# Two-layer hybrid decoder on one core: the SSM preparation's product on four column strips, and its kept matrices turned by DVE squares and DMAs instead of PE

## The chip, the cores and the metric

One core of a Trainium2 chip runs the whole kernel in one launch. The metric is the device time of that launch in microseconds, the median of three runs before. TensorE (PE) does the matmuls and has its own queue of weight loads (PEld); VectorE (DVE), ScalarE (ACT) and GpSimd (POOL) do the rest; SyncE (SP) issues nearly all DMAs. Each engine takes its instructions in the order in which they were emitted.

## What is computed

Two layers on x of 256 positions by 2048 columns. Each layer: RMSNorm, one input projection (2048 to 2816), three token mixers side by side, an output projection, a residual, RMSNorm, a SwiGLU feed-forward network of width 5632, a residual. The mixer that matters here is the SSM:

```
# per group g (32 groups of 16 channels, 64 complex states each)
s_t = Abar s_{t-1} + Bbar u_t          # Abar, Bbar from lam, dt, b only: no x in them
y_t = Re(C s_t) + D u_t
y   = gelu(y);  y = y * sigmoid(y @ w_glu)
```

## The kernel before

**Matmuls.** All large products are float32 split into two float32r parts. Weights stream from DRAM in 684 halves of 128x1024 (512 KB each) through five buffers ("raw"). ACT rounds a half to "whi" (L193), DVE makes the rest "wlo" (L203), and `unit` (L285 to L287) issues for each block of 128 input columns and each of two position blocks three matmuls of 512 columns: whi by xh, wlo by xh, whi by xl. A half is used up in two units.

**The order of the work.** One program order is written out in Python. `dense` emits one unit and then calls `tick` once. A tick gives each of the small tasks (generators) at most one step, six tasks per tick at most, the oldest first; `yield 0` means "go on at the next tick", `yield n` means n ticks later than that. Where a dense product needs something that a task has not emitted yet, `need` calls `tick` again and again with no dense unit between: below these are called empty ticks. The order in each engine's queue follows from this, and waits between engines are semaphores that the framework puts in.

**The SSM preparation, `ssm_prep(l, ct)`.** For each layer and each of four quarters ct of the groups it makes a "stash" of 3584 columns: wr and wi (each 512: block matrices turned by PE), m (512: the product of spread B and C powers, Toeplitz in blocks of four positions), gr, gn, cos, sin, d0. The turns are four PE transposes each (`turn`, L588), copied out by ACT at L622 and L637. The product is eight matmuls (L643) with 32 output rows each, `ps[0:32]`, at four column offsets, in two ticks of four; ACT then makes m with four copies (L651), shifted by 32 columns for each block of 32 rows. Only one preparation runs at a time (`prep_busy`).

Layer 0 prepares quarter 3 first and keeps it in DRAM (`saved`, L655), then quarters 0, 1 and 2, which stay in SBUF, all while the input projection runs. The four of layer 1 are prepared in the feed-forward network of layer 0, spaced by yields of 12 ticks (`slow`), and all kept in DRAM. `ssm_load` (L543) brings a kept stash back with one DMA of 1792 KB. So five of eight preparations are kept, and three are not.

**What uses the stash, `ssm_main(l, ct)`.** Eight matmuls with wr and wi (L683), DVE products and scans (L691 to L709), 12 matmuls with m, gr, gn (L716, L719, L721; float32, so each is two records in the trace), DVE (L728), gelu on ACT (L733), DVE squares (L736). Its yields add up to 19 ticks. `ssm_one` starts it when its preparation is done; quarter 3 is loaded when quarter 0's main is through.

**What waits for that.** The stash of quarter 1 lies in the buffer "ya" and that of quarter 2 in "yb". The attention task allocates "ya" for the output projection's input only when `main_done[1]` holds, so the first tile of the output projection follows the main of quarter 1 by four ticks. After four such tiles (16 units), `need(tssm)` at L1140 waits for all four mains and `glu_T`. The six input products before take 16 + 8 + 4 x 16 = 88 units.

Of the kernel before, what the change touches and what calls it, by code (L numbers as in the profile page):

```python
# [10 lines left out]
F32 = mybir.dt.float32  # L11
F32R = mybir.dt.float32r
AF = mybir.ActivationFunctionType
ALU = mybir.AluOpType

L = 2
# [142 lines left out]
class Builder:  # L159
# [380 lines left out]

    def ssm_load(self, l, ct):
        st = self.stash[(l, ct)] = self.ssm_store(ct)
        self.nc.sync.dma_start(out=st["all"], in_=self.saved[l][ct])  # L543
        yield 2

    def load_bc(self):
# [5 lines left out]
    def ssm_prep(self, l, ct, save=None):  # L552
        nc = self.nc
        v, pool = nc.vector, nc.gpsimd
        s0 = 16 * l + 4 * ct
        while self.prep_busy or not self.small_done:
            yield 0
        self.prep_busy = True
        st = self.stash[(l, ct)] = self.ssm_store(ct if save is None else 0 if l else 2)
        bc = self.bc  # L560
        slow = 12 if l else 0
        geng = pool if l else v
        c3 = lambda t, n: t[:, s0:s0 + 4].unsqueeze(2).to_broadcast([128, 4, n])
        v3 = lambda t: t.rearrange("p (a b) -> p a b", b=64)
        it = self.iota.unsqueeze(1).to_broadcast([128, 4, 64])
        cs = st["cs"]

        def cmul(eng, out, t, ar, pr, ai, pi, op, nq):

            sh = [128, 4, nq, 16]  # L570
            t, o = [z[:, 0:64 * nq].rearrange("p (a q b) -> p a q b", q=nq, b=16) for z in (t, out)]
            e = lambda a: a.unsqueeze(2).to_broadcast(sh)
            f = lambda p: p[:, s0:s0 + 4].unsqueeze(3).to_broadcast(sh)
            eng.tensor_tensor(out=t, in0=e(ai), in1=f(pi), op=ALU.mult)
            eng.tensor_tensor(out=o, in0=e(ar), in1=f(pr), op=ALU.mult)
            eng.tensor_tensor(out=o, in0=o, in1=t, op=op)

        def spread(out, src, n):

            o = out.rearrange("p (a b) -> p a b", b=32)  # L580
            i = src[:, 0:16 * n].rearrange("p (a b) -> p a b", b=16)
            for h in range(2):
                nc.scalar.activation(out=o[:, :, 16 * h:16 * h + 16], in_=i, func=AF.Copy, scale=self.half[:, h:h + 1])

        def turn(et):
            ps = yield from self.grab("side")
            for g in range(4):
                nc.tensor.transpose(ps[:, 128 * g:128 * g + 128], et[:, 128 * g:128 * g + 128], self.ident)  # L588
            return ps


        bb = self.work.tile([128, 2, 4, 16], F32, tag="bb", name="bb", bufs=1)
        t4 = st["gn"][:, 320:384].rearrange("p (a b) -> p a b", b=16)
        for o, p, q, op in ((0, 0, 1, ALU.subtract), (1, 1, 0, ALU.add)):
            pool.tensor_tensor(out=bb[:, o], in0=bc[:, p], in1=c3(self.cre, 16), op=ALU.mult)
            pool.tensor_tensor(out=t4, in0=bc[:, q], in1=c3(self.cim, 16), op=ALU.mult)
            pool.tensor_tensor(out=bb[:, o], in0=bb[:, o], in1=t4, op=op)
        cmul(pool, st["d0"], st["wi"][:, 256:512], bb[:, 0], self.per, bb[:, 1], self.pei, ALU.subtract, 4)
        yield 0
        cmul(geng, st["m"], cs, bc[:, 2], self.pfr, bc[:, 3], self.pfi, ALU.subtract, 5)  # L600
        cmul(pool, st["wr"], st["gn"], bc[:, 2], self.pfn, bc[:, 3], self.pfr, ALU.subtract, 5)
        cmul(pool, st["wi"][:, 0:256], st["wi"][:, 256:512], bb[:, 1], self.per, bb[:, 0], self.pei, ALU.add, 4)
        yield 1 + slow
        spread(st["gr"], st["m"], 20)
        yield 0
        et = self.work.tile([128, 512], F32, tag="et", name="et", bufs=1)
        spread(et, st["d0"], 16)
        f, g, h = cs[:, 256:512], cs[:, 0:256], st["m"][:, 0:256]
        v.tensor_tensor(out=v3(f), in0=c3(self.phh, 64), in1=it, op=ALU.mult)
        v.tensor_tensor(out=v3(g), in0=c3(self.phl, 64), in1=it, op=ALU.mult)  # L610
        yield 0
        ps = yield from turn(et)
        v.tensor_tensor(out=h, in0=f, in1=g, op=ALU.add)
        v.tensor_scalar(out=h, in0=h, scalar1=MAGIC, scalar2=MAGIC, op0=ALU.add, op1=ALU.subtract)
        yield slow
        spread(st["gn"], st["wr"], 20)
        self.load_bc()
        v.tensor_tensor(out=f, in0=f, in1=h, op=ALU.subtract)
        v.tensor_tensor(out=f, in0=f, in1=g, op=ALU.add)
        v.scalar_tensor_tensor(out=g, in0=f, scalar=-1.0, in1=f, op0=ALU.mult, op1=ALU.max)  # L620
        yield 0
        nc.scalar.activation(out=st["wr"], in_=ps, func=AF.Copy)  # L622
        self.drop("side")
        et = self.work.tile([128, 512], F32, tag="pt", name="et", bufs=1)
        spread(et, st["wi"], 16)
        yield 0
        nc.scalar.activation(out=st["sin"], in_=f, func=AF.Sin, scale=SIN_SCALE)
        nc.scalar.activation(out=st["cos"], in_=g, func=AF.Sin, scale=-SIN_SCALE, bias=self.hpi)
        yield slow
        ps = yield from turn(et)  # L630
        brep = self.work.tile([128, 2, 4, 32], F32, tag="et", name="brep", bufs=1)
        spread(brep.rearrange("p o a b -> p (o a b)"), bb.rearrange("p o a b -> p (o a b)"), 8)
        pool.memset(st["m"], 0.0)
        pool.tensor_copy(out=v3(st["d0"]), in_=c3(self.rho4, 64))
        pool.memset(v3(st["d0"])[:, :, 0:1], 0.0)
        yield 0
        nc.scalar.activation(out=st["wi"], in_=ps, func=AF.Copy)  # L637
        self.drop("side")
        yield slow
        ps = yield from self.grab("side")  # L640
        for g in range(4):
            for o, nm in ((0, "gr"), (1, "gn")):
                nc.tensor.matmul(out=ps[0:32, 128 * g:128 * g + 128], lhsT=brep[:, o, g],  # L643
                                 rhs=st[nm][:, 160 * g:160 * g + 128], start=(o == 0), stop=(o == 1))
            if g % 2:
                yield 0
        mv = st["m"].rearrange("p (g c) -> p g c", g=4)
        pv = ps.rearrange("p (g c) -> p g c", g=4)
        for q in range(4):
            p0 = 32 * q  # L650
            nc.scalar.activation(out=mv[p0:p0 + 32, :, p0:128], in_=pv[0:32, :, 0:128 - p0], func=AF.Copy)  # L651
        self.drop("side")
        if save is not None:
            yield 0
            nc.sync.dma_start(out=save, in_=st["all"])  # L655
        self.prep_busy = False
        yield 1

# [361 lines left out]
    def build(self):  # L1020
        nc = self.nc
# [50 lines left out]
        def prep0():  # L1072
            yield 15
            nc.vector.tensor_scalar(out=self.nsinks, in0=self.sinks, scalar1=-1.0, scalar2=None, op0=ALU.mult)
            nc.vector.tensor_scalar(out=self.sinks8, in0=self.sinks, scalar1=8.0, scalar2=None, op0=ALU.mult)
            yield from self.ssm_small()
            self.small_done = True
            yield from self.ssm_prep(0, 3, save=self.saved[0][3])

        self.saved = [[self.dram.tile([128, 3584], F32, name=f"saved{l}{ct}", tag=f"saved{l}{ct}") for ct in range(4)]  # L1080
                      for l in range(L)]
        self.spawn(prep0())

        for l in range(L):
# [30 lines left out]
            a = self.acc()  # L1115
            self.dense(a, self.X, D16, ready=ready)
            self.spawn(self.attn(l, 0, a, rs))
            a = self.acc()
            self.dense(a, self.X, D16, n=256)
            self.spawn(self.kv(a, rs))  # L1120
            a = self.acc()
            self.dense(a, self.X, D16)
            self.spawn(self.attn(l, 1, a, rs))
            a = self.acc()
# [3 lines left out]
            a = self.acc()  # L1128
            self.dense(a, self.X, D16)
            self.spawn(self.gmlp_v(l, a, rs))  # L1130
            a = self.acc()
# [6 lines left out]
            for t in out_tiles():  # L1138
                if t is None:
                    self.need(tssm)  # L1140
                    a = []
# [9 lines left out]
                f = n not in accs  # L1151
# [14 lines left out]
            for si, s in enumerate(FF_SETS):  # L1166
                self.hev = self.events()
                for i, c in enumerate(s):
                    a = self.acc()
                    self.dense(a, self.X, D16, ready=ready)  # L1170
                    tgte = self.spawn(self.ffn_h(c, i, a, None, rs))
                    a = self.acc()
# [10 lines left out]
                for n, part in down_parts(s):  # L1183
                    a = accs[n] if n in accs else self.acc()
# [57 lines left out]
        for m in range(2):  # L1242
            r = nrm["rs"][:, m:m + 1]
            t = self.work.tile([128, 2], F32, tag="ms", name="ms", bufs=4)
# [42 lines left out]
```

## Time and profile before

| | |
|---|---|
| median of 3 runs | 2032.88 us (2028.57, 2032.88, 2033.66) |
| the profiled execution | 2028.85 us, span 2027.1 us |
| PE busy, weight loads busy | 2003.0 us, 1668.5 us |
| DVE, ACT, POOL busy | 1201.4, 995.6, 155.9 us |

Busy time of PE contains the overlap of pipelined matmuls, so a matmul that lasts 0.39 us in the trace starts 0.23 us after the one ahead of it. Stages of the profiled execution: mixers of layer 0 up to about 230 us, feed-forward network up to about 1033 us, mixers of layer 1 up to about 1240 us, then the output projection and the second network.

### The profile page before, as it was taken

To read this page: it belongs to the slowest core of one execution; us is meant where nothing else is said; L and a number is where in the kernel's file an instruction comes from. 1 tells how busy PE (TensorE), PEld (TensorE's weight loads), DVE (VectorE), ACT (ScalarE), POOL (GpSimd) and SP (SyncE) were. 2 spreads that over 40 slices of the span, in tenths; PEclk is the share of its full clock that TensorE was granted. 3 is DMA by queue.
4 is the path that set the end of the run, shared out by engine and by line. 5 is a ranking of instruction groups with operands and counts; after the bars stand their busy time and mean duration, and the time that the engine had idled before them with its cause. 6 is when DMAs were issued, how large, how long until landed. Compare 5 with 4: busy or idle time off the path is not lost.

```text
span 2027.1 us, 25451 instructions
## 1 busy us (share of the span) xinstructions
PE 2003.0 (99%) x9456; PEld 1668.5 (82%) x9456; DVE 1201.4 (59%) x1673; ACT 995.6 (49%) x1367; POOL 155.9 (8%) x204
## 2 busy tenths in 40 slices
PE   8999999999999999999999999999999999999998
PEld 7888888888888888888888888888888888888886
DVE  6868775555546555455675796655555555555555
ACT  6776554545445444444455445544443444434443
POOL 0342003020303000000000010000000000000000
PEclk9999999999999999999999999999999999999999
DMA  7533477666656666566776356766665666666664
GB/s 251 174 131 138 154 256 232 222 229 224 223 202 232 235 226 204 193 218 211 252 254 231 108 197 207 240 221 215 216 211 196 208 219 217 213 192 201 225 218 146
DMA packets 127773, 422.63 MB, mean 208 GB/s; under 512 B 15008, under 2 KB 31008, under 8 KB 126368
## 3 DMA queue, kind: packets, MB, share of 16 engines
q1 hardware_dynamic: 125632, 416.69, 61.2%
q0 software_dynamic: 1152, 3.15, 0.6%
q8 instruction: 74, 1.21, 0.2%
q10 hardware_dynamic: 864, 1.16, 0.2%
q14 instruction: 51, 0.42, 0.1%
HBM read 391.84 MB, written 29.10 MB: 208 GB/s over the span
## 4 chain that ended last, share of the span: by engine, by line
PE 94%; DVE 3%; ACT 1%; issue 1%; DMA 1%; SPq 0%; POOLq 0%; POOL 0%; DVEq 0%; ACTq 0%
PE acc L285 29%; PE acc L287 29%; PE acc L286 29%; PE side L909 1%; DVE wlo L203 1%; PE side L643 1%; PE side L683 1%; PE side L875 1%; PE side L899 0%; PE side L349 0%; PE side L721 0%; PE side L719 0%; DVE st L691 0%; PE side L716 0%; PE side L588 0%
## 5 line engine op out<-in xcount | busy, mean ns | idle before, releaser
L203 DVE TENSOR_TENSOR wlo<-raw,whi 128x1024 fp32r<-128x1024 f32 (+1 forms) x687 | 846.1, 1240 | 629.3 <-ACT whi L193 625.4
L193 ACT ACTIVATE whi<-raw 128x1024 fp32r<-128x1024 f32 (+1 forms) x687 | 724.8, 1056 | 957.3 <-PE acc L287 901.7
L285 PE MATMUL acc<-whi,xh 128*128 128x512 f32 (+1 forms) x1792 | 699.9, 391 | 2.9 <-ACT whi L193 1.8
L287 PE MATMUL acc<-whi,xl 128*128 128x512 f32 (+1 forms) x1792 | 692.1, 386 | 0.0
L286 PE MATMUL acc<-wlo,xh 128*128 128x512 f32 (+1 forms) x1792 | 691.8, 386 | 0.1
L285 PEld LDWEIGHTS acc<-whi,xh 128*128 128x128 f32 x1792 | 337.1, 188 | 69.5 <-ACT whi L193 2.2
L287 PEld LDWEIGHTS acc<-whi,xl 128*128 128x128 f32 x1792 | 337.0, 188 | 68.5
L286 PEld LDWEIGHTS acc<-wlo,xh 128*128 128x128 f32 x1792 | 337.3, 188 | 65.2 <-DVE wlo L203 0.8
L285 PE MATMUL acc<-whi,ya 128*128 128x512 f32 x512 | 200.5, 392 | 0.0
L286 PE MATMUL acc<-wlo,ya 128*128 128x512 f32 x512 | 199.3, 389 | 0.3 <-DVE wlo L203 0.3
L287 PE MATMUL acc<-whi,ya 128*128 128x512 f32 x512 | 199.3, 389 | 0.0
L285 PE MATMUL acc<-whi,yb 128*128 128x512 f32 x448 | 175.0, 391 | 0.0
L287 PE MATMUL acc<-whi,yb 128*128 128x512 f32 x448 | 174.4, 389 | 0.0
L286 PE MATMUL acc<-wlo,yb 128*128 128x512 f32 x448 | 174.3, 389 | 0.0
L286 PEld LDWEIGHTS acc<-wlo,ya 128*128 128x128 f32 x512 | 96.2, 188 | 20.2 <-DVE wlo L203 0.7
L287 PEld LDWEIGHTS acc<-whi,ya 128*128 128x128 f32 x512 | 96.1, 188 | 20.1
L285 PEld LDWEIGHTS acc<-whi,ya 128*128 128x128 f32 x512 | 96.2, 188 | 19.7 <-issue 0.2
L287 PEld LDWEIGHTS acc<-whi,yb 128*128 128x128 f32 x448 | 84.1, 188 | 17.6
L285 PEld LDWEIGHTS acc<-whi,yb 128*128 128x128 f32 x448 | 84.1, 188 | 17.4 <-issue 0.2
L286 PEld LDWEIGHTS acc<-wlo,yb 128*128 128x128 f32 x448 | 84.1, 188 | 17.3
L1248 POOL TENSOR_TENSOR rs<-ms,nh 128x1 f32<-128x1 f32 x2 | 1.8, 924 | 699.9 <-DVE ms L1246 699.9
L371 POOL DMA_DIRECT2D turned<-turn x24 | 13.5, 564 | 511.5 <-DVE turn L366 511.4
(251 smaller groups left out, 1196.5 us busy)
## 6 DMA issues: line engine op xcount, KB each, us to landing
raw<-wts SPq DMA_DIRECT2D x684, 512.0 KB, 4.2
quad<-turned SPq DMA_DIRECT2D x34, 512.0 KB, 5.0
turned<-turn SPq DMA_DIRECT2D x112, 128.0 KB, 3.9
saved<-stash SPq DMA_DIRECT2D x4, 1792.0 KB, 6.7
stash<-saved SPq DMA_DIRECT2D x3, 1792.0 KB, 7.6
stashb<-saved SPq DMA_DIRECT2D x2, 1792.0 KB, 9.3
turned<-turn POOLq DMA_DIRECT2D x24, 128.0 KB, 3.9
saved<-stashb SPq DMA_DIRECT2D x1, 1792.0 KB, 6.6
```

The costliest lines, as they stand in the source:

```text
L193: self.nc.scalar.activation(out=h[:, o:o + w], in_=self.raw[j][:, o:o + w], func=AF.Copy)
L203: self.nc.vector.tensor_tensor(out=o[:, i:i + w], in0=r[:, i:i + w], in1=self.hi[j][:, i:i + w], op=ALU.subtract)
L285: nc.tensor.matmul(out=o, lhsT=a, rhs=wh, start=first, stop=False)
L286: nc.tensor.matmul(out=o, lhsT=a, rhs=wl, start=False, stop=False)
L287: nc.tensor.matmul(out=o, lhsT=b, rhs=wh, start=False, stop=last)
L371: queue.dma_start(out=d[:, :, a].rearrange("b j f -> j b f"), in_=t[32 * a:32 * a + 32].rearrange("p (b f) -> p b f", b=4))
L643: nc.tensor.matmul(out=ps[0:32, 128 * g:128 * g + 128], lhsT=brep[:, o, g], rhs=st[nm][:, 160 * g:160 * g + 128], start=(o == 0), stop=(o ...
L683: nc.tensor.matmul(out=ps[:, 256 * o + 64 * g:256 * o + 64 * g + 64], lhsT=st[nm][:, 128 * g:128 * g + 128], rhs=U4[:, 4 * ct + g, :])
L875: nc.tensor.matmul(out=ps[:, nk * i:nk * i + nk], lhsT=qT[:, h0 + i], rhs=self.kT[:, j, cq, 0:nk], start=(j == 0), stop=(j == 1))
L909: nc.tensor.matmul(out=ps[:, 64 * i:64 * i + 64], lhsT=pT[:, 128 * (nb * i + b):128 * (nb * i + b) + 128], rhs=self.v[:, b, 64 * cq:64 * c ...
L1248: nc.gpsimd.tensor_tensor(out=r, in0=t[:, 0:1], in1=self.nh[:, 0:1], op=ALU.pow)
```

## The change

The product's four blocks of rows go to PSUM partitions 0, 32, 64 and 96 (`ps[32g:32g+32, 0:128]`), first all four with gr, then all four with gn, in one tick. One ACT copy of 128x128 moves the result into columns 96 to 223 of m, whose first 96 columns are zero. Four DMAs write it to DRAM, each read from a place shifted by 32 columns, so that the shift of m arises there; for an unkept quarter one more DMA brings m back into SBUF, and the preparation waits four ticks longer for that. For a kept quarter PE does not turn wr and wi: DVE turns 32x32 squares (one instruction of 128x512 each), and eight DMAs, two ticks apart, put blocks of squares in their places in DRAM; gr to d0 go with one DMA as before. `ssm_load` takes three DMAs: two for wr and wi out of the turned blocks, one for the rest.

```diff
 def ssm_load(self, l, ct):
     st = self.stash[(l, ct)] = self.ssm_store(ct)
-    self.nc.sync.dma_start(out=st["all"], in_=self.saved[l][ct])
+    save, turns = self.saved[l][ct]
+    for o in range(2):
+        self.nc.sync.dma_start(out=st["all"][:, 512 * o:512 * o + 512],
+                               in_=turns[o].rearrange("c (q g) s -> q c (g s)", q=4))
+    self.nc.sync.dma_start(out=st["all"][:, 1024:3584], in_=save)
     yield 2
 ...
     def turn(et):
+        if save is not None:
+            return None
 ...
+    def turned(nm, ps, et):
+        if save is None:
+            nc.scalar.activation(out=st[nm], in_=ps, func=AF.Copy)
+            self.drop("side")
+            return
+        v.transpose(out=st[nm].rearrange("p (q g j) -> p g q j", q=4, g=4),
+                    in_=et.rearrange("p (g q j) -> p g q j", g=4, q=4))
 ...
-        nc.scalar.activation(out=st["wr"], in_=ps, func=AF.Copy)
-        self.drop("side")
+        turned("wr", ps, et)
 ...
-        pool.memset(st["m"], 0.0)
+        pool.memset(st["m"][:, 0:96], 0.0)
 ...
-        nc.scalar.activation(out=st["wi"], in_=ps, func=AF.Copy)
+        turned("wi", ps, et)
+        yield slow
+        ps = yield from self.grab("side")
+        for o, nm in ((0, "gr"), (1, "gn")):
+            for g in range(4):
+                nc.tensor.matmul(out=ps[32 * g:32 * g + 32, 0:128], lhsT=brep[:, o, g],
+                                 rhs=st[nm][:, 160 * g:160 * g + 128], start=(o == 0), stop=(o == 1))
+        yield 0
+        nc.scalar.activation(out=st["m"][:, 96:224], in_=ps[:, 0:128], func=AF.Copy)
         self.drop("side")
-        yield slow
-        ps = yield from self.grab("side")
-        for g in range(4):
-            for o, nm in ((0, "gr"), (1, "gn")):
-                nc.tensor.matmul(out=ps[0:32, 128 * g:128 * g + 128], lhsT=brep[:, o, g],
-                                 rhs=st[nm][:, 160 * g:160 * g + 128], start=(o == 0), stop=(o == 1))
-            if g % 2:
-                yield 0
-        mv = st["m"].rearrange("p (g c) -> p g c", g=4)
-        pv = ps.rearrange("p (g c) -> p g c", g=4)
+        yield 1
+        if save is None:
+            rows = self.dram.tile([128, 512], F32, tag="rows", name="rows", bufs=2)
+        else:
+            save, turns = save
+            rows = save[:, 0:512]
         for q in range(4):
-            p0 = 32 * q
-            nc.scalar.activation(out=mv[p0:p0 + 32, :, p0:128], in_=pv[0:32, :, 0:128 - p0], func=AF.Copy)
-        self.drop("side")
-        if save is not None:
-            yield 0
-            nc.sync.dma_start(out=save, in_=st["all"])
+            nc.sync.dma_start(out=rows[32 * q:32 * q + 32].rearrange("c (g t) -> g c t", g=4),
+                              in_=st["m"][:, 96 - 32 * q:224 - 32 * q])
+        if save is None:
+            yield 2
+            nc.sync.dma_start(out=st["m"], in_=rows)
+        else:
+            for o in (0, 512):
+                for a in range(4):
+                    nc.sync.dma_start(out=turns[o // 512][:, :, 32 * a:32 * a + 32],
+                                      in_=st["all"][32 * a:32 * a + 32, o:o + 512].rearrange("c (r j) -> c r j", j=32))
+                    yield 1
+            nc.sync.dma_start(out=save[:, 512:2560], in_=st["all"][:, 1536:3584])
         self.prep_busy = False
         yield 1
```

## Rows read from the trace of the kernel before

**Rows 1.** The page: busy time by engine, granted clock, chain that ended last.

```profile
PE 2003.0 (99%) x9456; PEld 1668.5 (82%) x9456; DVE 1201.4 (59%) x1673; ACT 995.6 (49%) x1367; POOL 155.9 (8%) x204
...
PEclk9999999999999999999999999999999999999999
...
PE 94%; DVE 3%; ACT 1%; issue 1%; DMA 1%; SPq 0%; POOLq 0%; POOL 0%; DVEq 0%; ACTq 0%
```

**Rows 2.** Windows by stage: length, busy time by engine, clock, DMA share, GB/s.

```profile
60.00:205.00 145.00, 138.39 (x837) 117.51 (x836) 111.84 (x269) 104.44 (x217) 45.72 (x65) 1.00 0.43 146
...
355.00:700.00 345.00, 345.00 (x1559) 283.19 (x1559) 190.03 (x190) 171.75 (x218) 50.45 (x66) 1.00 0.66 224
```

**Rows 3.** Timeline of PE around one turn: start, length, engine, line, operation.

```profile
402.68 0.39 PE L287 MATMUL acc<-whi,xl 128*128 128x512 f32 x1
402.91 0.60 PE L588 MATMUL side<-ident,et 128*128 128x128 f32 x4
403.27 0.48 PE L285 MATMUL acc<-whi,xh 128*128 128x512 f32 x1
403.58 0.40 PE L286 MATMUL acc<-wlo,xh 128*128 128x512 f32 x1
```

**Rows 4.** Timeline of PE around one half of the product.

```profile
422.21 0.39 PE L287 MATMUL acc<-whi,xl 128*128 128x512 f32 x1
...
422.53 1.06 PE L643 MATMUL side<-stash,brep 128*32 128x128 f32 x8
...
423.52 0.50 PE L285 MATMUL acc<-whi,xh 128*128 128x512 f32 x1
...
423.86 0.40 PE L286 MATMUL acc<-wlo,xh 128*128 128x512 f32 x1
```

**Rows 5.** Lines L588 and L643: count, shortest, median and longest, first and last.

```profile
L588 PE MATMUL side<-ident,et x64: 270/272/328, 71.7 to 666.4; 128*128 128x128 f32 x64
...
L643 PE MATMUL side<-stash,brep x80: 272/273/297, 116.2 to 689.1; 128*32 128x128 f32 x80
```

**Rows 6.** Timeline of PE where the output projection of layer 0 begins.

```profile
190.00 1.89 PE L683 MATMUL side<-U,stashb 128*128 128x64 f32 x16
...
193.02 0.55 PE L349 MATMUL side<-ident,yattn 128*128 128x128 f32 x3 [0.71 <-ACT yattn L779]
193.40 1.06 PE L958 MATMUL side<-t,wst 128*128 128x128 f32 x8
194.29 1.04 PE L349 MATMUL side<-ident,yattn 128*128 128x128 f32 x8
196.06 1.97 PE L683 MATMUL side<-U,stash 128*128 128x64 f32 x16 [0.73 <-DVE ya L431]
197.84 0.48 PE L285 MATMUL acc<-whi,ya 128*128 128x512 f32 x1
```

**Rows 7.** Groups by line: DVE's squares, count, busy us, mean ns, idle before.

```profile
L366 DVE STREAM_TRANSPOSE turn<-t 128x512 f32<-128x512 f32 x44 | 28.5, 684 | 0.0
```

**Rows 8.** Timeline of PE: half of a main's second product.

```profile
181.92 0.39 PE L716 MATMUL side<-U,stashb 128*128 128x64 f32 x2
...
183.24 0.48 PE L285 MATMUL acc<-whi,xh 128*128 128x512 f32 x1
```

**Rows 9.** DMA issues: count, KB each, median us from issue to landing.

```profile
raw<-wts SPq DMA_DIRECT2D x684, 512.0 KB, 4.2
...
turned<-turn SPq DMA_DIRECT2D x112, 128.0 KB, 3.9
saved<-stash SPq DMA_DIRECT2D x4, 1792.0 KB, 6.7
stash<-saved SPq DMA_DIRECT2D x3, 1792.0 KB, 7.6
```

**Rows 10.** Timeline of SP: layer 1's load of quarter 3 is issued.

```profile
1180.93 0.42 SPq L543 DMA_DIRECT2D stash<-saved  x1
```

**Rows 11.** Timeline of PE: layer 1's main of quarter 3 begins.

```profile
1189.65 1.89 PE L683 MATMUL side<-U,stash 128*128 128x64 f32 x16
```

More of the change, by code (lines that the diff above doesn't have):

```diff
@@ L636, in ssm_prep @@
         yield 0
-        nc.scalar.activation(out=st["wi"], in_=ps, func=AF.Copy)
-        self.drop("side")
+        turned("wi", ps, et)
         yield slow
         ps = yield from self.grab("side")
-        for g in range(4):
-            for o, nm in ((0, "gr"), (1, "gn")):
-                nc.tensor.matmul(out=ps[0:32, 128 * g:128 * g + 128], lhsT=brep[:, o, g],
+        for o, nm in ((0, "gr"), (1, "gn")):
+            for g in range(4):
+                nc.tensor.matmul(out=ps[32 * g:32 * g + 32, 0:128], lhsT=brep[:, o, g],
                                  rhs=st[nm][:, 160 * g:160 * g + 128], start=(o == 0), stop=(o == 1))
-            if g % 2:
-                yield 0
-        mv = st["m"].rearrange("p (g c) -> p g c", g=4)
-        pv = ps.rearrange("p (g c) -> p g c", g=4)
-        for q in range(4):
-            p0 = 32 * q
-            nc.scalar.activation(out=mv[p0:p0 + 32, :, p0:128], in_=pv[0:32, :, 0:128 - p0], func=AF.Copy)
-        self.drop("side")
-        if save is not None:
-            yield 0
-            nc.sync.dma_start(out=save, in_=st["all"])
+        yield 0
+        nc.scalar.activation(out=st["m"][:, 96:224], in_=ps[:, 0:128], func=AF.Copy)
+        self.drop("side")
+        yield 1
[4 more added lines that the diff above has]
+            rows = save[:, 0:512]
+        for q in range(4):
+            nc.sync.dma_start(out=rows[32 * q:32 * q + 32].rearrange("c (g t) -> g c t", g=4),
[10 more added lines that the diff above has]
+            nc.sync.dma_start(out=save[:, 512:2560], in_=st["all"][:, 1536:3584])
         self.prep_busy = False
@@ L1078, in prep0, with kept @@
             yield from self.ssm_prep(0, 3, save=self.saved[0][3])
-        self.saved = [[self.dram.tile([128, 3584], F32, name=f"saved{l}{ct}", tag=f"saved{l}{ct}") for ct in range(4)]
-                      for l in range(L)]
+        def kept(l, ct):
+            a = self.dram.tile([128, 2560], F32, name=f"saved{l}{ct}", tag=f"saved{l}{ct}")
+            b = self.dram.tile([2, 32, 16, 128], F32, name=f"turns{l}{ct}", tag=f"turns{l}{ct}")
+            return a, b
+        self.saved = [[kept(l, ct) for ct in range(4)] for l in range(L)]
         self.spawn(prep0())
```

## The prediction, made before the change was run

> **What bounds the kernel now.** I read the page first: PE is busy for 99% of the span at the full granted clock, and 94% of the chain that ended last is PE, while DVE is busy for 59% and ACT for 49% [rows 1]. The windows by stage come next, and there the reader is to see two different stages. In the feed-forward network of layer 0 (355 to 700 us, where the four preparations of layer 1 run) PE is never idle, so each microsecond of its work that goes is a microsecond of the span. In the mixers of layer 0 (60 to 205 us, where the four preparations of layer 0 run) PE is idle for 145.0 - 138.4 = 6.6 us, and DVE and ACT are busy for more than 70% [rows 2]; there work is bound by chains as well. The third view is the timeline of PE around the edited operations, and the fourth that of the place where the output projection begins.
>
> **Turns that go (five preparations, two each).** Matmuls of 512 columns start 0.23 us apart. The turn lets the next one start at 403.27, where 402.91 would have been its time, so 0.36 us; the one behind it then starts 0.31 instead of 0.23 us later, since its weights were not loaded ahead: 0.08 more [rows 3]. A turn costs 0.44 us of PE. Eight of the ten lie in the network: 8 x 0.44 = 3.5 us. The two of layer 0 give 0.9 us.
>
> **The product (eight preparations).** Half of it is eight records between 422.21 and 423.52, 1.31 us where 0.23 is usual, and the next start is again 0.34 instead of 0.23 us later: 1.08 + 0.11 = 1.19 us per half, 2.38 us per preparation [rows 4]. The eight records span 1.06 us, of which the last takes 0.27 by itself [rows 5], so they start (1.06 - 0.27)/7 = 0.11 us apart and fill 0.88 us; 0.31 us of a half is entering and leaving that form of tile. The new product has 16 records in one group, so 0.31 is paid once. No row shows matmuls on two strips side by side, because all records of before write the same 32 rows. The bounds: nothing overlaps, 0.31 + 16 x 0.11 = 2.07 us, a gain of 0.31; or four strips at once, 0.31 + 4 x 0.11 = 0.75 us, a gain of 1.63. I take a value between: a float32 matmul is two records on the same strip, the second has to follow the first, and starts are in order, so if strips do run beside each other only the second record of one pair and the first of the next can share the time. That is nine steps, 0.31 + 9 x 0.11 = 1.30 us, a gain of 1.08 us per preparation. Four in the network: 4.3 us (1.2 to 6.5). Four in layer 0: the same.
> The Trainium skill, page "TensorE: Matmul & The Clock Gate", section "Part 3: Packing small matmuls", gives 2.38 times for three strips with 512 columns; by that, as an estimate, the 16 records would fill 0.74 us and the gain would be 1.33 us. No row here shows it.
>
> **The network as a whole.** PE gains 3.5 + 4.3 = 7.8 us there (4.7 to 10.0). What hides the new work: two DVE squares of 0.68 us per preparation [rows 7] against two ACT copies that go, on a DVE that is busy 190 of 345 us [rows 2]; a remainder that comes 1 us late still has the two halves of weights (2 x 2.72 us) that DVE works ahead. The DMAs on SP: four of 64 KB for m and eight of 64 KB in pieces of 128 bytes, two ticks (2.72 us) apart. A DMA of 128 KB in pieces of 1 KB lands in 3.9 us [rows 9]; the new ones have half the bytes and four times the pieces, so between 3.9 us and, by pieces alone, 15.6 us. I take the low end, nearest in bytes. A weight half behind one on SP lands in 4.2 us, while five buffers give 5 x 2.72 = 13.6 us; that is the cover, and without it each late half would cost what exceeds 9.4 us. The preparations end 4 x 16 ticks later (87 us), long before layer 1 loads them. So nothing is added here.
>
> **Layer 0, where the change also makes a chain longer.** Counting yields: quarter 3 frees the next preparation 3 ticks after its product before, and 19 after the change (ACT, two ticks, eight DMAs two ticks apart): +16. Quarters 0 and 1 each finish 4 ticks later (the store of m, three ticks, the load). The main of quarter 1 starts when its preparation is done, so it and `main_done[1]` come 16 + 4 + 4 = 24 ticks later. The first tile of the output projection waits for that already: before, nine empty ticks lie between the last unit on X and the first on ya, and they take 197.84 - 190.00 = 7.84 us, 0.87 us each. They hold 52 records (two first products of mains, 12 turns, of which the rows show eleven, and eight of L958) x 0.11 = 5.7 us of PE work, so PE loses only 2.1 us [rows 6]. After the change there are 33 empty ticks. At 0.87 us they last 28.7 us; I take 30, since the chain in them now holds a DRAM round trip (its price is with the rivals). But the work in them is work taken out of the units before: 48 records of L683, 72 of the second products (12 in 183.24 - 181.92 = 1.32 us, 0.11 each [rows 8]), 8 of turns, 28 as before, 156 x 0.11 = 17.2 us, and two products of 1.30: 19.8 us. PE loses 30 - 19.8 = 10.2 us, 8.1 more than before. The units ahead become lighter, and I give back half of the 6.6 us of idle PE [rows 2]: 3.3. Net +4.8 us. The gains of layer 0 are 0.9 + 4.3 = 5.2 us. Layer 0 thus comes out at -0.4 us. The second wait, at `need(tssm)`, moves along: its last main is then 28 ticks later, four more than the first tile, against six empty ticks now, in which other work has gone; I cost it at nothing. The round trip of m (3.9 us to land and, as an estimate, as much to come back) lies within the ticks that I counted; for quarter 2 five units cover it.
>
> **The sum.** -7.8 - 0.4 = -8.2 us. Against the profiled execution's own 2028.85 us that is 2020.7; that execution is one of the fast ones and lies 4.0 us below the median of three, whose runs differ by 5.1 us. Against the median: 2024.7 us.
>
> **The rivals.**
> *Strips run one after another.* The product gains 0.31 eight times, 2.5 instead of 8.6 us: -2.1 us, 2030.8 us, no measurable change. For it: records of one strip do follow at 0.11 us. Against it: those had no choice.
> *The empty ticks fill up.* If the 30 us shrink to the 20 us of work in them, PE loses nothing there: -8.2 - 10.2 = -18 us, about 2014 us. For it: before, 5.7 of 7.84 us were work. Against: the chain alternates DVE, PE and ACT with one quarter left in flight.
> *The load on few rings.* The load of wr and wi now reads DRAM in an outer dimension of four. If transfers are dealt out by it, each of four rings carries 128 KB for wr and wi where the whole old load put 112 KB on each of 16, and 208 KB with the rest: 7.6 us x 208/112 = 14.1 us [rows 9]. In layer 1 quarter 3's main starts 8.7 us after its load was issued [rows 10, 11], so PE waits 0 to 5.4 us: up to 2030.1 us, no measurable change. The Trainium skill, page "DMA: Bandwidth & Descriptors", section "Why a DMA increments its semaphore by 16 and not by 1", has this rule: the number of engines is the largest that divides the slowest dimension of both sides. No row here shows it.
> *Slower: the longer chain in layer 0.* Place: the empty ticks before the first output tile. If one costs 1.36 us, as much as a unit, instead of 0.87, the wait is 45 us, PE loses 15 us more than I take, and the sum is +6.8 us: 2039.7 us. It becomes slower than before once an empty tick exceeds (30 + 8.2)/33 = 1.16 us. For it: the chain now holds a DRAM round trip, which empty ticks of before do not, and SP waits for its landing. Against it: before's ticks held two mains as well.
>
> **How the numbers follow.** About 0.3% (6.1 us) is what a measurement can tell from no change. The forecast with its neighbours 0.48, strips one after another 0.15, the ticks filled 0.10, the few rings 0.10, slower 0.12, and 0.05 for a loss below 6.1 us by the same chain. Faster by over 0.3%: most of the forecast's own cases and the filled ticks, 0.55. Within 0.3%: the serial strips, the few rings, the small loss and what of the forecast falls short of 6.1 us, 0.33. Slower: 0.12. The range takes in the filled ticks, the strips in a row and the small loss, over runs that differ by 5 us: 2013 to 2037.
>
> **What would show it.** L588 falls from 64 to 24 records; L643 stays at 128, in groups of 16 that take about 1.3 us of PE from the last dense matmul to the next, not 2.07 or 0.75. The 355 to 1033 us stage becomes 7.8 us shorter. At the first output tile PE's timeline shows some 30 us without a dense matmul, two thirds of it busy. The prediction is wrong if that gap passes 38 us, if weight halves land late in the network, or if PE waits there for DVE.

## The result: slower by 0.9%, and the profile after

The changed kernel takes 2051.36 us (median of 6 runs, 2048.67 to 2055.16) against 2033.21 us of the kernel before on the same chip (6 runs): a ratio of 1.0093 [1.0082, 1.0104], 18 us more, where 8 us less was forecast. The profiled execution took 2048.67 us, with a span of 2046.7 us.

Of the page of the changed kernel, the rows that answer to [rows 1]:

```profile
PE 2004.7 (98%) x9416; PEld 1671.1 (82%) x9416; DVE 1209.9 (59%) x1683; ACT 984.7 (48%) x1336; POOL 151.6 (7%) x204
...
PEclk9997799999999999999999999999999999999999
...
PE 92%; DVE 3%; ACT 2%; DMA 1%; issue 1%; SPq 1%; POOL 0%; POOLq 0%; DVEq 0%; ACTq 0%
```

PE has 40 records fewer and is busy 1.7 us longer; the reason stands in the row of the clock: in the fourth and fifth slice the granted clock, which was full everywhere before, is at 0.7. To see where the time lies, the start of the k-th dense unit after is set against that of the k-th before. A dense unit is counted here as the three matmuls of one position block (half of what `unit` emits), from 0:

| dense unit | stage | after minus before, us |
|---|---|---|
| 176 | input projection of layer 0, its last tenth | -19.4 |
| 192 | first unit of the output projection | +31.9 |
| 400 | feed-forward network begins | +25.9 |
| 900 | in the network | +15.0 |
| 1000 | end of the network | +17.2 |
| 1570 | layer 1, after quarter 3's main | +19.5 |
| 2767 | end | +20.4 |

So there are four places: layer 0 loses 25.9 us, the network gains 10.8 up to unit 900 and gives back 2.2 behind it, layer 1 loses 1.9 at quarter 3. The rest (1.3 us) is less than runs of one kernel differ by.

**Layer 0.** Busy time from 60 us to unit 400, a windows row of before and then the same of after (columns as in [rows 2]):

```profile
60.00:349.40 289.40, 282.69 (x1502) 237.64 (x1501) 209.22 (x418) 181.30 (x328) 70.50 (x94) 1.00 0.54 179
```

```profile
60.00:375.20 315.20, 293.46 (x1496) 248.31 (x1495) 212.85 (x420) 179.66 (x317) 67.49 (x94) 0.92 0.53 169
```

PE idles 315.20 - 293.46 = 21.7 us where it idled 6.7: 15.0 of the 25.8 us. The other 10.8 are busy time: six records fewer, and yet 10.8 us more. A windows table of the stretch between the last unit on X and the first on ya shows why:

```profile
160.00:170.00 10.00, 9.19 (x80) 8.24 (x79) 6.99 (x17) 6.51 (x12) 5.55 (x12) 1.00 0.25 80
170.00:180.00 10.00, 2.25 (x11) 1.64 (x9) 7.92 (x27) 7.67 (x19) 3.68 (x7) 0.57 0.12 39
180.00:190.00 10.00, 9.36 (x74) 8.68 (x75) 6.61 (x20) 6.60 (x16) 0.00 (x0) 0.75 0.16 36
190.00:200.00 10.00, 6.67 (x33) 6.04 (x31) 4.96 (x20) 7.31 (x12) 1.27 (x1) 0.59 0.83 247
200.00:210.00 10.00, 5.80 (x26) 5.61 (x26) 8.26 (x16) 1.15 (x2) 5.47 (x3) 0.50 0.09 34
210.00:220.00 10.00, 8.69 (x40) 8.51 (x40) 8.78 (x27) 1.45 (x3) 0.00 (x0) 0.50 0.01 2
220.00:230.00 10.00, 8.81 (x41) 8.19 (x41) 5.53 (x17) 4.73 (x10) 0.70 (x1) 0.53 0.00 0
```

From 170 us, where PE was busy for 2.25 us of ten, the granted clock is between 0.75 and 0.50; 0.50 is the lower level, 1.2 GHz. From 210 to 230 us PE is busy for 87% with some 40 records in 10 us, where [rows 6] has 52 in 7.84. The timeline of PE in the same gap of after, with the idle time before an instruction and its releaser in brackets:

```profile
194.24 3.62 PE L708 MATMUL side<-U,stashb 128*128 128x64 f32 x16
...
205.16 0.63 PE L741 MATMUL side<-U,stashb 128*128 128x64 f32 x2
210.74 0.69 PE L744 MATMUL side<-stashb 128*128 128x63 f32 x2 [4.95 <-DVE stashb L716]
...
223.14 2.02 PE L983 MATMUL side<-t,wst 128*128 128x128 f32 x8
...
229.69 0.47 PE L285 MATMUL acc<-whi,ya 128*128 128x512 f32 x1
```

L708 is the old L683 and L983 the old L958: sixteen records take 3.62 us where [rows 6] has 1.89, eight take 2.02 where it has 1.06. The gap lasts from 162.6 to 229.69 us, 67.1 us with 284 records; before it was 7.84 us with 52. What PE waited for in it (total, times, longest):

```profile
PE side L934 <- DVE pT L929: 6.2, 3, 2.9
PE side L594 <- ACT et L587: 5.5, 1, 5.5
PE side L744 <- DVE stashb L716: 4.9, 1, 4.9
PE side L349 <- ACT yattn L804: 1.2, 2, 0.6
```

These are a preparation (L594), a main (L744) and the attention (L934): parts of three chains, each handing over between PE, ACT and DVE. None of them waits for a DMA.

**The network.** A product there, timeline of PE, to be set beside [rows 4]:

```profile
768.15 0.39 PE L287 MATMUL acc<-whi,ya 128*128 128x512 f32 x1
768.47 0.65 PE L657 MATMUL side<-stash,brep 128*32 128x128 f32 x16
769.04 0.50 PE L285 MATMUL acc<-whi,ya 128*128 128x512 f32 x1
```

Sixteen records span 0.65 us, less than the 1.06 us of eight in [rows 4]. In the trace the sixteen start in fours: four within 0.02 us, the next four 0.13 us after the first, and two more rounds 0.11 us apart. Over all of the network, each step from one dense start to the next that exceeds the usual 0.227 us was added up by what stands beside it: before, turns 3.62 us and products 9.53; after, turns 0 and products 3.12. Per preparation, the turns that went cost 0.90 us, and the product costs 0.78 us where it cost 2.38 with one strip. After has 1.56 us more at seven other steps, 1.27 of it at one place near 782 us. (By these steps the network gains 10.0 us and loses 1.6, 8.6 net as in the table of units. Of the 2.2 us that the table shows behind unit 900, 0.78 is no loss: the last product, ahead of unit 900 before, stands behind it after.) At that place the timeline of SP (issue times) and the waits of ACT and PE show:

```profile
772.68 1.53 SPq L669 DMA_DIRECT2D saved<-stash  x1
774.25 1.66 SPq L677 DMA_DIRECT2D turns<-stash  x1
776.01 0.62 SPq L184 DMA_DIRECT2D raw<-wts  x1
776.68 0.43 SPq L377 DMA_DIRECT2D quad<-turned  x1
```

```profile
ACT yb L386 <- DMA quad<-turned: 1.7, 1, 1.7
```

```profile
PE acc L285 <- ACT yb L386: 0.7, 1, 0.7
```

SP takes 1.5 to 1.7 us to issue each of two of the new DMAs there; the load of the next turned block ("quad", the input of a dense product) stands behind them and comes 1.7 us late for ACT, and PE waits. That the issue times make it late is argued from this order; no run shows it by itself. In layer 1 the waits of PE at quarter 3's main say `stash<-turns`, the turned load, 1.6 us.

### The profile page after: what moved, and what is told of

It is laid out like the page before. It is cut to its first block, busy times and chain, and to the rows that moved or that the text cites. A ratio compares the mean times of both kernels' runs of the same rounds, so it can differ in the third digit from the quotient of the medians.

```text
span 2046.7 us, 25461 instructions
## 1 busy us (share of the span) xinstructions
PE 2004.7 (98%) x9416; PEld 1671.1 (82%) x9416; DVE 1209.9 (59%) x1683; ACT 984.7 (48%) x1336; POOL 151.6 (7%) x204
## 3 DMA queue, kind: packets, MB, share of 16 engines
q10 hardware_dynamic: 864, 1.16, 0.2%
## 4 chain that ended last, share of the span: by engine, by line
PE 92%; DVE 3%; ACT 2%; DMA 1%; issue 1%; SPq 1%; POOL 0%; POOLq 0%; DVEq 0%; ACTq 0%
PE acc L285 29%; PE acc L287 29%; PE acc L286 29%; PE side L934 1%; PE side L900 1%; DVE wlo L203 1%; DVE st L716 1%; PE side L349 0%; DMA stash<-turns 0%; DMA quad<-turned 0%; PE side L924 0%; PE side L708 0%; ACT whi L193 0%; ACT sc L919 0%; ACT L919 0%
## 5 line engine op out<-in xcount | busy, mean ns | idle before, releaser
L285 PEld LDWEIGHTS acc<-whi,yb 128*128 128x128 f32 x448 | 84.1, 188 | 18.5 <-ACT yb L386 1.3
```

The lines of the kernel that those rows point to most:

```text
L285: nc.tensor.matmul(out=o, lhsT=a, rhs=wh, start=first, stop=False)
```

## Experiments

The order of emission can be counted: the changed kernel has 51 empty ticks at the first output tile, not the 33 of the prediction. `main_done[1]` comes where the prediction had it, but the cap of six steps per tick also held up the attention tasks, which end at tick 121 instead of 84 before. So the experiments had three readings to tell apart: the cap (starved tasks), the longer order itself, and the price of the new operations (squares, DMAs, strips).

**The cap lifted.** In the changed kernel:

```diff
-    def tick(self, cap=6):
+    def tick(self, cap=12):
```

> The changed kernel with at most twelve steps of tasks per tick instead of six; every operation is the same, only the order moves. Theory 1 (empty ticks: polling tasks used up the six steps, the attention tasks behind them starved, and PE stood without dense units for 51 ticks instead of the 33 that the longer preparation alone explains): the emission order then has 33 empty ticks; 18 fewer at 67/51 = 1.3 us give back about 20 to 24 us, 2027 to 2031 us. Theory 2 (the gap is made by DMA round trips of m and by the lower clock of PE, whatever the count of ticks): the gap stays above 60 us, 2045 us or more.

Measured: 2048.33 us, 1.0077 [1.006, 1.0093]. Its gap, from the last unit on X to the first on ya, as a windows row:

```profile
172.22:219.06 46.84, 36.59 (x193) 34.06 (x193) 32.08 (x76) 21.12 (x41) 16.01 (x24) 0.56 0.26 76
```

The empty ticks are 33, as predicted, and the gap is 46.8 us instead of 67.1, but unit 400 still starts 24.4 us late (25.9 in after). Of the 20.2 us by which the gap is shorter, the units ahead of it, between which the tasks now stand, take 9.6, and the sixteen behind it 7.3, part of them at a granted clock of 0.50 (229 to 239 us). Neither theory fits: the first misses the time, and the second, which has it, said that the gap stays above 60 us. Starvation is real and costs nearly nothing here: as the main cause it falls.

**The lock freed before the eight DMAs.** In the changed kernel, in layer 0 alone:

```diff
+            if l == 0:
+                self.prep_busy = False
             for o in (0, 512):
                 for a in range(4):
```

> The changed kernel, but in layer 0 the kept quarter frees the next preparation before its eight turn DMAs instead of after them. Theory 1: 18 empty ticks instead of 51; PE's loss in the gap, 38 us, falls to 5 to 8 us; 2018 to 2024 us. Theory 2 (round trips of m, three of them, unchanged here): the gap loses only the 16 ticks x 0.9 us of waiting, about 2037 us.

Measured: 2032.68 us, 1.0004 [0.9995, 1.0013]. All operations are there; only the sixteen ticks for which the next preparation had to wait are gone, and with them 18.7 us between the medians, 16.7 of it by unit 400. The gap is 33.3 us with 18 empty ticks, and the time is above what theory 1 gave.

**One half of the change each.** First before's product with squares and DMAs, then before's turns and single load with the new product and m's way through DRAM:

```diff
 e_turns_only: after, but
-   ps[32 * g:32 * g + 32, 0:128] ...; four stores of m
+   ps[0:32, 128 * g:128 * g + 128] ...; four ACT copies of m as before
 e_strips_only: after, but
-   v.transpose(out=st[nm] ...); eight DMAs; three loads
+   four PE transposes, one ACT copy; two stores; one load
```

> The kernel before with only the turning part of the change: kept wr and wi by DVE squares and eight DMAs two ticks apart; the product as before on one strip in two halves. Theory 1: 43 empty ticks against 9 before; the network gains about 3.5 us only; 2045 to 2050 us. Theory 2 (the DRAM round trip of m is what costs): no round trip here, so the gap stays small, 2027 to 2033 us.

> The kernel before with only the product's part of the change: four strips, m through DRAM; wr and wi of kept quarters turned by PE and kept by plain DMAs without yields between them. Theory 1: 17 empty ticks; PE loses 5 to 8 us there instead of 2, the network gains about 6.5 us; 2024 to 2031 us. Theory 2: three round trips of m as in the changed kernel, so most of the gap stays, 2045 us.

Measured: turns alone 2060.49 us, 1.014 [1.0125, 1.0155]; strips alone 2036.70 us, 1.0024 [1.0013, 1.0034]. In the network the two gains are 3.6 and 6.3 us, and they add. In layer 0 both lose, 31.7 and 10.8 us, with 43 and 17 empty ticks at the first tile; these losses do not add (both together lose 25.9). Turns alone has no way of m through DRAM and is still the slowest of the three: theory 2, that this way is what costs, falls. Strips alone also loses 4.8 us at one place of layer 1 (its timeline of PE):

```profile
1052.69 0.39 PE L287 MATMUL acc<-whi,xl 128*128 128x512 f32 x1
1056.12 0.79 PE L285 MATMUL acc<-whi,xh 128*128 128x512 f32 x1 [3.04 <-ACT xh L390]
1056.71 0.63 PE L286 MATMUL acc<-wlo,xh 128*128 128x512 f32 x1
1057.14 0.63 PE L287 MATMUL acc<-whi,xl 128*128 128x512 f32 x1
1057.57 0.63 PE L285 MATMUL acc<-whi,xh 128*128 128x512 f32 x1
```

After 3.04 us without work dense matmuls start 0.43 us apart instead of 0.23, at a granted clock of 0.50. ACT itself waited there for the load of a turned block (`quad<-turned`), 4.1 us where it waited 2.1 in before; why that load was later is open.

**The order alone.** The kernel before, its operations untouched, with nothing but more yields in layer 0:

```diff
         if save is not None:
             yield 0
+            if l == 0:
+                yield 15
             nc.sync.dma_start(out=save, in_=st["all"])
+        else:
+            yield 3
```

> The kernel before with nothing but yields added: in layer 0 the kept preparation holds the lock 16 ticks longer and the others 4 each, as in the changed kernel; no operation is added, removed or altered. Theory 3 (the order alone: a preparation and two mains move into a stretch without dense units, and there PE drops to the lower clock): the loss of layer 0 appears by itself, 20 to 25 us, 2052 to 2058 us. Theory 4 (the new DMAs and the trip of m through DRAM make the gap long): at most 5 to 8 us, below 2040 us.

Measured: 2048.71 us, 1.0083 [1.0068, 1.0098]; unit 400 starts 22.9 us late. No DMA, square or strip is added, and nearly nine tenths of layer 0's loss are there, with the same fall of the clock. Windows row from 60 us to unit 400:

```profile
60.00:372.30 312.30, 296.90 (x1508) 250.90 (x1507) 213.13 (x418) 181.62 (x328) 68.68 (x95) 0.94 0.49 166
```

PE idles 15.4 us (8.7 more than before) and is busy 14.2 us longer, for the same work. This shows the cause of most of the loss in layer 0: the place of the preparations in the order.

**The tail as a task of its own.** After, with the lock freed in layer 0 as soon as ACT has moved the product; stores, load and turned DMAs follow in a separate task, for which a main's second product waits; then the same with each turned load of 128 partitions cut in four of 32:

```diff
+        if l == 0:
+            self.prep_busy = False
+            st["tail"] = self.spawn(tail())
```

```diff
-            nc.sync.dma_start(out=st["all"][:, 512 * o:512 * o + 512],
-                              in_=turns[o].rearrange("c (q g) s -> q c (g s)", q=4))
+            for q in range(4):
+                nc.sync.dma_start(out=st["all"][32 * q:32 * q + 32, 512 * o:512 * o + 512],
+                                  in_=turns[o][:, 4 * q:4 * q + 4].rearrange("c g s -> c (g s)"))
```

> The changed kernel, but in layer 0 the lock is freed as soon as ACT has moved the product, and the stores, the load of m and the turn DMAs go on as a task of their own. Theory 3: 11 and 7 empty ticks (9 and 6 before), the gap is back near 10 us, layer 0 is within 3 us of before, the network keeps its 8 to 11 us, layer 1 loses 2 to 5 us at quarter 3's load: 2024 to 2031 us. Theory 4: the three trips of m remain, 2040 us or more.

> As e_tail, and each of the two loads of turned blocks is cut into four DMAs of 32 partitions, so that the outer dimension is 32 on both sides instead of 4 and 128. If few rings made quarter 3's load late, PE's wait for it in layer 1 (1.9 to 5 us) goes, and the time is 2 to 5 us below e_tail; if the load is late for its bytes, the two are the same.

Measured: 2039.56 us, 1.0032 [1.002, 1.0044], and 2034.65 us, 1.0013 [1.0003, 1.0024]. Freeing the lock still earlier did not help further: with 11 empty ticks, near before's 9, the gap is 18.5 us with 60 records at a clock of 0.66, and layer 0 loses 13.6 us. A PE idle of 3.6 us ahead of a turn comes at 121.8 us besides, with the clock at 0.50 from 125.1 to 132.0 us. Why eleven ticks cost 18.5 us here and nine 7.84 before, the timeline of PE in the gap shows in part:

```profile
196.04 0.33 PE L349 MATMUL side<-ident,yattn 128*128 128x128 f32 x1 [2.44 <-ACT yattn L818]
203.03 0.69 PE L758 MATMUL side<-stashb 128*128 128x63 f32 x2 [3.30 <-DVE stashb L728]
```

PE idles 7.2 us in it, 1.5 in before's. Before's ticks held first products of two mains; these hold second products, which wait for DVE's work on a main (3.9 us in all), and turns that wait for the attention's output from ACT (3.1, against 0.7). From 196.8 us the clock is 0.50, with PE busy for 8.1 us. So an empty tick has no price of its own: it costs what the handovers in it and the clock make it.

The cut load shows cleanly. Waits of PE from 1175 to 1235 us in the first of the two:

```profile
PE side L720 <- DMA stash<-turns: 2.0, 1, 2.0
```

In the second there is no such row, and the step from unit 1540 to unit 1570 is 4.55 us shorter, the same as before's to 0.01 us. The lost time is more than the wait that the row shows, since the dense units behind it are slow too (clock 0.50 from 1200.3 to 1207.2 us). The packets of the DMAs show the load itself: the 256 packets of 2 KB that carry wr and wi take 7.6 us in after, at most six of them under way at a time; with the cut load they take 3.7 us, with up to 18.

**The new DMAs of layer 1 on POOL.**

```diff
-   nc.sync.dma_start(out=turns ...)
+   (nc.gpsimd if l else nc.sync).dma_start(out=turns ...)
```

> As e_tail_load8, and in layer 1 the four stores of m and the eight turn DMAs of a kept preparation are issued by POOL instead of SP. If SP's issue times (0.6 to 1.7 us each) made the quad load of the network late, the 2 us lost near 780 us go; if not, no difference, or a loss where POOL issues slowly.

Measured: 2060.77 us, 1.0141 [1.0125, 1.0156], 26 us more than with SP. Waits of DVE from 470 to 500 us, and of PE from 485 to 500 us:

```profile
DVE stash L625 <- POOL stash L581: 12.9, 1, 12.9
```

```profile
PE acc L286 <- DVE wlo L203: 7.8, 1, 7.8
```

And the timeline of POOL, the last of the eight DMAs and the first product behind it:

```profile
485.70 0.63 POOL L683 DMA_DIRECT2D turns<-stash  x1 [3.83 <-issue]
486.35 0.30 POOL L611 TENSOR_TENSOR bb<-bc,cre 128x64 f32<-128x64 f32 x1
```

POOL also computes in the preparation. Its queue holds the eight DMAs, 3.4 to 5.9 us apart, so the next preparation's POOL products start late; DVE waits for them with wlo behind that wait, and PE stands for 7.8 us. This happens in three of the four preparations (22.5 us of PE in all). So this run does not test what it was meant to test, whether SP's issue times cost the 2 us near 780.

**A filler in the gap.** After, with four matmuls of 256 columns that nobody reads in 44 of the 51 empty ticks:

```diff
-                self.need(ready[k])
+                while not ready[k]["done"]:
+                    if xs is self.Y and first and i == 0:
+                        ... four matmuls of X by X into a free side bank
+                    self.tick()
```

> The changed kernel, and in 44 of its 51 empty ticks ahead of the first output-projection unit TensorE gets four extra matmuls of 256 columns into a side bank that nobody reads (176 records, about 0.11 us each at the upper clock, 19 us in all). Nothing else differs; the order of all other work and its chain are the same. Theory clock (the gap of 67.3 us is as long as it is because the granted clock falls to 0.50 while dense work pauses, so that its records and everything that waits for them run at half speed): with the filler the clock stays near 1.00 in the gap, the kernel's own records there need about 25 us instead of 45, and the gap shrinks in spite of 19 us more work, to 45 to 52 us; the time is 2030 to 2037 us. Theory chain (the ticks take this long because of DVE, ACT and their handovers, the clock is a by-product): the gap stays at 67 us or grows by up to the filler's 19 us, whatever the clock; 2051 to 2070 us.

Measured: 2053.64 us, 1.0106 [1.0092, 1.012]. The windows row of the gap, of after and then with the filler:

```profile
162.62:229.69 67.07, 47.84 (x286) 44.52 (x284) 46.43 (x132) 32.51 (x68) 16.67 (x23) 0.62 0.20 59
```

```profile
161.90:232.01 70.11, 61.42 (x462) 58.55 (x460) 45.96 (x132) 32.58 (x69) 16.77 (x23) 0.85 0.19 57
```

The clock rises from 0.62 to 0.85, but the gap does not shrink: 70.1 us is what the chain reading expected, and the clock reading's 45 to 52 us is missed by far. The rows say more than that. In after's gap the clock is at 0.50 from 171.41 to 185.07 and from 191.89 us on, and PE is busy for 35.4 us of this; as records there last 3.62 instead of 1.89 us, some 17 us of it are lost to the clock, as an estimate, and 19.2 us of the gap are idle. With the filler PE is busy for 18.5 us at 0.50, some 9 us lost, and 8.7 us are idle. The filler halves both losses, some 18.6 us together, and its 176 records cost more than that, since the gap is 3.0 us longer. So the gap is not made by the clock alone, as the clock reading had it, and buying the clock back with empty work is no gain. That the slow clock costs PE time is shown (records of twice the length, with PE busy for 87% from 210 to 230 us in after); how much shorter the gap would be at full clock no run isolates.

**The change in layer 1 alone.** Layer 0 wholly as before; squares, DMAs and strips in the network, with the cut load; and the same with more ticks between the stores:

```diff
     def turn(et):
-            if save is not None:
+            if l:
                 return None
 ...
+        if l == 0:
+            ...                                   # product, copies and store of before
+        else:
+            ...                                   # product, stores and DMAs of after
 # e_l1_wide, layer 1: three more ticks after each store of m, one more after each turned DMA
```

> Layer 0 wholly as in the kernel before (PE turns, one-strip product, one keeping store and one load of quarter 3); the change only in the four preparations of layer 1 in the network, with each of the two turned loads cut in four of 32 partitions. If the loss of the change is all in layer 0 (order and clock) and in the uncut load, and the network's part is a gain as the prediction had it, then before the network 0 against the kernel before, 8.6 us gained in the network (10.8 from turns and products, 2.2 lost to SP's late DMAs), 0 at layer 1's quarter 3: 2023 us (2021 to 2026), below both kernels. The prediction's own network term gives 2024 (2022 to 2027). If the network's gain were given back in layer 1 by the matrices being kept in DRAM, 2031.

> As the one before, with two ticks instead of none between the four stores of m and two instead of one between the eight stores that turn, in layer 1. If the 2.2 us lost in the network come from these twelve issues standing together on SP ahead of the block DMA of the dense units' sums, spacing them brings 1 to 2.2 us: 2021 us (2019 to 2024). If the loss has another place, or the lock held 15 ticks longer delays a preparation that somebody waits for, no gain or a loss: 2023 to 2030.

Measured: 2020.99 us, 0.9945 [0.9933, 0.9957], and 2022.59 us, 0.9955 [0.9942, 0.9969]. The first beats both kernels, by 11 and by some 30 us. Its page, and the end of its gap:

```profile
PE 1995.0 (99%) x9424; PEld 1662.0 (82%) x9424; DVE 1206.7 (60%) x1681; ACT 986.4 (49%) x1347; POOL 155.6 (8%) x204
...
PEclk9999999999999999999999999999999999999999
```

```profile
191.72 1.89 PE L724 MATMUL side<-U,stashb 128*128 128x64 f32 x16
...
197.78 1.97 PE L724 MATMUL side<-U,stash 128*128 128x64 f32 x16 [0.74 <-PE side L349]
199.56 0.48 PE L285 MATMUL acc<-whi,ya 128*128 128x512 f32 x1
```

The gap is 7.84 us with 52 records at full clock, as [rows 6]; the network gains 9.4 us, and PE has no wait at all between 1160 and 1190 us. Wider spacing brought nothing that can be measured. ACT still waited for the turned block, 3.9 us in two places between 690 and 840 us, where the closer spacing had 0.9: there the block's own stores, right behind the last keeping store, took up to 1.50 us each to issue, against 0.43 to 0.49. The crowd on SP had moved, and PE lost 2.6 us in the network beside the products instead of 0.8.

The gaps of nine kernels, by the windows row from the end of the last unit on X to the first on ya:

| kernel | empty ticks | gap us | records | PE busy us | clock | unit 400, us |
|---|---|---|---|---|---|---|
| before | 9 | 7.84 | 52 | 6.3 | 1.00 | 0 |
| layer 1 alone | 9 | 7.84 | 52 | 6.3 | 1.00 | +1.8 |
| tail as a task | 11 | 18.5 | 60 | 11.3 | 0.66 | +13.6 |
| strips alone | 17 | 30.4 | 104 | 19.3 | 0.62 | +10.8 |
| lock freed before the DMAs | 18 | 33.3 | 116 | 21.7 | 0.62 | +9.1 |
| order alone | 33 | 46.3 | 168 | 32.3 | 0.63 | +22.9 |
| cap 12 | 33 | 46.8 | 192 | 36.6 | 0.56 | +24.4 |
| turns alone | 43 | 67.6 | 268 | 50.9 | 0.63 | +31.7 |
| after | 51 | 67.1 | 284 | 47.8 | 0.62 | +25.9 |

A tick of the small gap takes 0.87 us; in every longer gap one takes 1.3 to 1.9 us. Each of these gaps has a clock of 0.56 to 0.66, and the two of 7.84 us have 1.00. (The 1.8 us of layer 1 alone lie ahead of its gap, where the clock is at 0.50 from 177.5 to 181.0 us.)

## Why the prediction was wrong, step by step

**The turns: right.** 0.44 us each was taken, 3.5 us in the network; the steps beside turns add up to 3.62 us, and squares and DMAs alone gain 3.6. L594 has 24 records, as predicted.

**The product: mechanism between the bounds, size wrong.** 1.08 us per preparation was taken, with the ends 0.31 and 1.63. Measured is (9.53 - 3.12)/4 = 1.60 us: the end with four strips at once. The argument that failed here is that only the neighbours of two pairs can share the time. In the row of L657, 0.65 - 0.27 us (the last record by itself, [rows 5]) leave 0.38 us between the first and the last start: sixteen records in four rounds of four, 0.11 to 0.13 us apart. Which record of a round lies on which strip the trace does not name. The Trainium skill, page "TensorE: Matmul & The Clock Gate", section "Part 3: Packing small matmuls", would have given 1.33 us as an estimate; the trace shows 1.60, with four strips and 128 columns instead of three and 512.

**The network: right within its range.** -7.8 us was forecast (4.7 to 10.0); measured is 8.65 net, 10.0 gained at turns and products by the steps, and some 1.5 lost. What was costed at nothing there was SP: one of its new DMAs took up to 1.66 us to issue, and by the order on its queue a turned block came late. The cover named, five buffers of weights, held for the weights (ACT waited for them 8.3 us in five places, before and after alike); the turned blocks of the down product were not named.

**The load on few rings: right as a rival, in place and size.** 0 to 5.4 us at layer 1's quarter 3 was given; 1.9 us in after, 4.6 with the tail as a task, 5.9 with the filler, and it goes to 0 when the load is cut in pieces of 32 partitions, whose packets run up to 18 at a time instead of six. This fits the rule of the Trainium skill given in the prediction (page "DMA: Bandwidth & Descriptors", section "Why a DMA increments its semaphore by 16 and not by 1"): the uncut load has an outer dimension of four, the cut one of 32.

**Layer 0: the step that failed.** -0.4 us was forecast and +25.9 measured. The place was right (the first output tile), and so was the count of the chain (33 ticks, as cap 12 has them; the changed kernel itself has 51). Wrong was the price of an empty tick. 0.87 us was read off a gap of 7.84 us, in which the clock was full, and 30 us taken for 33 such ticks; with those 33 ticks the gap lasts 46.8 us, 1.42 us each. PE is idle in it for 10.2 us, just what was forecast, and busy for 36.6 us where 19.8 were taken: all of the 16.8 us that this gap was missed by is busy time. The granted clock, of which the prediction said nothing, accounts for it: it is at 0.50 from 177.83 to 218.79 us, and PE is busy for 34.8 us of that. At 3.62 us for 1.89, as an estimate, 16.7 us of these are lost to the clock, and 19.9 us of work remain, which is what was taken. The slower rival (1.36 us per tick, a gap of 45 us, 2039.7 us, decided from 1.16 us) had place and size of the gap, with another mechanism: it named the DRAM round trip, and order alone makes a gap of 46.3 us without one.

That the time is 2051 and not 2040 has two further parts. The 18 ticks of starved attention, which the count had left out, made the gap 20 us longer and took nearly as much out of the units around it: cap 12 is three microseconds faster by the medians, 1.5 at unit 400. And the gains of layer 0 (5.2 us by the prediction) and the 3.3 us of idle time given back did not appear: the preparations run in stretches where PE isn't the bound, so what they no longer ask of PE is no time saved. This last point is argued from the idle time of 21.7 us and from two runs with 33 empty ticks each: cap 12, with the new operations, starts unit 400 24.4 us late, the order alone, without them, 22.9. No run isolates it.

**What would show it.** "Wrong if that gap passes 38 us" was the sentence that decided: it was 67.1. Weight halves came no later than before, and PE did not wait for DVE in the network of the changed kernel; it did with the DMAs on POOL.

## What to carry to other kernels

A gap that is filled with small chained matmuls is priced by a row from a gap of its own length: read the granted clock in it, since in the gaps of 18 to 67 us here it was 0.56 to 0.66 on the mean, and a record at 0.50 took twice its time. Where one generator holds a lock, every yield behind the last useful operation is delay for the next one; here sixteen idle ticks cost as much as the whole change. And a change that pays where PE is the bound can be made there alone: in the network alone it brought 11 us, in the mixers nothing but a longer chain.

## What was not expected of the hardware

- Four column strips run side by side: 16 float32 records of 128 columns start in fours and take 0.65 us, one strip needed 1.06 us for eight.
- After 3.04 us without a matmul, dense matmuls start 0.43 us apart instead of 0.23; in the gap records took 3.62 us for 1.89, at a granted clock of 0.50.
- The stores that turn, in pieces of 128 bytes, took SP 0.55 to 1.66 us each to issue (0.56 in the median), against 0.42 us for the whole load of [rows 10].
- Cutting two loads of 128 partitions in four of 32 each took 4.55 us off the path in layer 1; the time of their packets fell from 7.6 to 3.7 us.
